# Delta-rule loop of a hybrid decoder trunk: the hand-written order changed around the gated halves, the bonus, the weight rows and the last two tiles

## The chip, the cores and the metric

The kernel runs on one core of a Trainium2 chip. The core has a matrix engine (PE, TensorE), whose weight loads the profile lists apart as PEld, and three engines for elementwise work: DVE (VectorE), ACT (ScalarE) and POOL (GpSimd). SP (SyncE) issues nearly all transfers between the main memory and the on-chip SBUF. PE writes into PSUM banks, which DVE and ACT empty. Each engine works through its own list of instructions in order, and semaphores hold an instruction until what it reads is there. The metric is the device time in microseconds (us) of one execution.

## The reference

Two layers act on x (1024 tokens by 1024 channels, float32). The first is an RWKV-7 time mixer: after projections, a state of 64 by 64 for each of 16 heads is carried over all tokens by a delta rule, its outputs are normalised by head, a bonus is added, and the sum is gated and projected. The second layer is a differential attention; each layer ends with a gated per-layer input. The part that the change touches:

```python
def step(state, inp):
    r_t, w_t, k_t, v_t, kk_t, b_t = inp
    sa = jnp.einsum('bhij,bhj->bhi', state, kk_t)
    state = (state * w_t[:, :, None, :] - sa[..., None] * b_t[:, :, None, :]
             + v_t[..., None] * k_t[:, :, None, :])
    y_t = jnp.einsum('bhij,bhj->bhi', state, r_t)
    return state, y_t
...
y = (y - mean) * lax.rsqrt(var + GN_EPS) * ln_w + ln_b
y = (y + bonus).reshape(B, S, RW_WIDTH)
return (y * jax.nn.silu(gate)) @ w_out
```

## The kernel before, in words

Every matrix product keeps float32 accuracy by splitting both operands into a rounded half ("h") and a rest ("l") and running three matmuls (`mm3`: h by h, h by the weight's l, l by the weight's h). `split` makes the halves: ACT writes the rounded one, then DVE or POOL subtracts it from the source.

The delta rule is run in 16 chunks of 64 tokens, by a loop over c near the end of the function `trunk`. In a chunk PE multiplies the state (tiles `xy`), ACT copies the result to `x`, PE makes `u`, DVE makes `vu` from it, PE makes `s`, DVE adds it to the decayed state (`state`), and PE finishes `xy`, from which ACT copies the outputs `y`. The next chunk's operands are prepared beside it by two units (st 0 and 1): transfers `kkr` and `kb` bring them in, POOL multiplies (`kbp`, `pr`, and a mask on half of `m`), PE transposes (`kbt`) and multiplies (`pm`, `prt`), ACT and DVE empty PSUM (`kbn`, `m`, `bon`). A unit's `kb` buffer is loaded again once POOL's `pr` has read it.

What fills PE between these small products are dense pieces: in chunks 0 to 3 a projection of the per-layer input (`pps`), later the output projection of a finished tile of 128 tokens (`op`), in eight pieces of six matmuls, four pieces a chunk. They are handed out by `more()`. A tile is two chunks. Its steps are spread over the chunks that follow: in an even chunk load, mean (`norm`), square, `bonus_v` (POOL, tile `vn`); in the odd chunk sums, roots, `scaled` (DVE, then POOL's `y<-y,lnw`), `added` (DVE's `y<-y,vn`, the bonus), and `turn(0)` (PE transposes half the tile into `ytr`, DVE gates it into `sg`); in the next even chunk `turned` (ACT rounds `gh<-sg`, DVE makes `gl`), `turn(1)` and `turned` again, and then the first `op` pieces, which read `gh` and `gl`. The eight rows of the output weight are split inside the loop too (`wo_row`: a transfer `rwoNr`, ACT's `rwoNh`, DVE's `rwoNl`).

While the loop is written, `pin` is set: PE, DVE, ACT and POOL keep the order of the code. SP, and everything after the loop, is placed by a scheduler, which may also put later, unpinned instructions between pinned ones. After the loop come the steps of the last two tiles (6 and 7), the gate weights' rows (`pwg`), and the first normalised tile of the next stage (`n`, transposed into `ptr`), whose products are `pg`. All operations are recorded through a wrapper at line 50, so tiles and not lines tell them apart.

Of the kernel before, what the change touches and what calls it, by code (L numbers as in the profile page):

```python
# [37 lines left out]
def trunk(ctx: ExitStack, tc: tile.TileContext, A, out):  # L38
# [814 lines left out]
    def big(kt, x, nm, dt=F32R):  # L853
        return dw.tile([P, D], dt, tag=f"b{kt}{x}", name=nm, bufs=1)

    with NB("d") as d, NP("psco") as pp:
# [55 lines left out]
        def chain_u(c):  # L912
            vu2, px, spl, x = ctx_c[0]
            ti = tis[c // 4]
            pu = [pp.tile([P, 4, 2, L], F32, tag="us", name=f"u{st}_{c}", bufs=2) for st in range(2)]
            ms = []
            if True:
                for p_ in range(4):
                    for h in range(2):
                        for st in (1, 0):  # L920
                            xs_ = half_(st)
                            ms.append(T.matmul(pu[st][xs_, p_, h], lhsT=ti[xs_, (c % 4) * 8 + h * 4 + p_],
                                               rhs=x[xs_, h, p_], start=True, stop=True))
            turns(ms)
            for st in range(2):
                xs_ = half_(st)
                V.tensor_tensor(out=vu2[xs_, st], in0=pu[st][xs_],
                                in1=rn[xs_, c].rearrange("p h j -> p j h").unsqueeze(3).to_broadcast([64, 4, 2, L]),
                                op=ALU.mult)
# [23 lines left out]

        D1, wo = {}, {}

        def wo_row(kt):
            tags = ("sq", "xr", (6, 0), (6, 1), "sq", "xr", (7, 0), "sq")
            tg, nm = tags[kt], f"rwo{kt}r"
            r = dt_(tg, nm) if isinstance(tg, str) else big(*tg, nm, F32)
            nc.sync.dma_start(out=r, in_=A["rwo"][:, kt])  # L960
            h, lo = big(kt, 0, f"rwo{kt}h"), big(kt, 1, f"rwo{kt}l")
            split(h, lo, r, V)
            wo[kt] = (h, lo)
# [123 lines left out]
        for c in range(NCH):  # L1087
# [23 lines left out]
            unit("load", 0, 1)  # L1111
            if odd and w:
                w["sums"]()
            chain_x(c)
            unit("decayed", 0)
            if pj and not odd:
                pj["turned"]()
                pj["turn"](1)
            if w and odd:
                w["roots"]()  # L1120
# [7 lines left out]
                wo_row(0)  # L1128
            if c == 2:
                wo_row(5)  # L1130
            chain_u(c)
            if w:
                w["scaled" if odd else "load"]()
# [6 lines left out]
            unit("pr", 0, 1)  # L1140
            if c == 1:
                wo_row(1)
            chain_s(c)
            if c == 1:
                wo_row(4)
            if c == 3:
                more(9)
                for kt in (2, 3, 6, 7):
                    wo_row(kt)
            if w and not odd:  # L1150
                w["squares"]()
                w["bonus_v"]()
            more(2)
            unit("turn", 1)
            if w and odd:
                w["added"]()
                w["turn"](0)
            more(9)
            unit("bonus", 1)
            if c == 12:  # L1160
                early_raw()
            if c == 13:
                early_row(0)
                early_row(1)
        for e in engines:
            e.pin = False
        co_cm.__exit__(None, None, None)
# [70 lines left out]
            for f in pieces:  # L1238
                f()

        t6, t7 = tile_(NT - 2), tile_(NT - 1)
        tile_(NT - 3)["squares1"]()
        t6["turned"]()
        t6["turn"](1)
        t6["turned"]()
        run(t6["m0"])
        run([t7[nm] for nm in ("load", "norm", "squares", "bonus_v", "sums", "roots", "scaled", "added")])
        while len(wg) < 6:
            gate_w()
        run(t6["m1"])  # L1250
        t6["squares1"]()
        pre2(0)
        gate_w()
# [463 lines left out]
```

## Time and profile before

| what | value |
|---|---|
| median of three runs | 1818.96 us (1814.44 to 1821.0) |
| the profiled execution's own time | 1819.65 us |
| its span, first to last instruction | 1817.8 us |
| mean granted PE clock over the span | 0.959 |
| PE busy in the span | 1683.5 us (93%) |
| the loop over chunks in the profile | from 575 to 882 us |

The span and the time lie 1.85 us apart. A stretch in which PE has nothing in flight is idle time, listed in brackets behind the instruction that ended it with the name of what it waited for. The granted clock is 1.00 at 2.4 GHz and 0.50 at 1.2 GHz; a mean between them over a stretch says how much of it ran at either. A window's row gives its bounds, its length, the busy time of PE, PEld, DVE, ACT and POOL (with the number of instructions), the mean granted clock, and the DMA engines' share and rate.

### The profile page before, as it was taken

To read this page: it belongs to the slowest core of one execution; us is meant where nothing else is said; L and a number is where in the kernel's file an instruction comes from. 1 tells how busy PE (TensorE), PEld (TensorE's weight loads), DVE (VectorE), ACT (ScalarE), POOL (GpSimd) and SP (SyncE) were. 2 spreads that over 40 slices of the span, in tenths; PEclk is the share of its full clock that TensorE was granted. 3 is DMA by queue.
4 is the path that set the end of the run, shared out by engine and by line. 5 is a ranking of instruction groups with operands and counts; after the bars stand their busy time and mean duration, and the time that the engine had idled before them with its cause. 6 is when DMAs were issued, how large, how long until landed. Compare 5 with 4: busy or idle time off the path is not lost.

```text
span 1817.8 us, 31112 instructions
## 1 busy us (share of the span) xinstructions
PE 1683.5 (93%) x11768; PEld 1393.4 (77%) x11768; DVE 1268.2 (70%) x2910; ACT 799.4 (44%) x1690; POOL 608.4 (33%) x647
## 2 busy tenths in 40 slices
PE   6899999898999979898799899899999999999998
PEld 5677778887677867777678678788888888777786
DVE  7865846697993556555856737787877878856765
ACT  6567733246254433334424334444444444544332
POOL 4433635123324444546400332333323323321200
PEclk9999999998898979999899999999999999999999
DMA  7115544534226643353533310101101101431122
GB/s 260 50 54 163 149 116 99 139 100 113 64 74 191 184 137 117 122 164 95 196 116 116 126 35 30 53 24 38 56 7 56 53 10 56 155 99 34 59 93 70
DMA packets 164403, 176.02 MB, mean 97 GB/s; under 512 B 74845, under 2 KB 127837, under 8 KB 164254
## 3 DMA queue, kind: packets, MB, share of 16 engines
q1 hardware_dynamic: 161950, 169.84, 30.2%
q10 hardware_dynamic: 2304, 4.20, 0.6%
q8 instruction: 93, 1.52, 0.3%
q14 instruction: 56, 0.46, 0.1%
HBM read 124.19 MB, written 49.81 MB: 96 GB/s over the span
## 4 chain that ended last, share of the span: by engine, by line
PE 53%; DVE 7%; ACT 1%; DMA 1%; issue 1%; POOL 0%; SPq 0%; DVEq 0%; ACTq 0%; POOLq 0%
PE qkv L50 18%; PE fg L50 5%; PE do L50 4%; PE pg L50 4%; PE op L50 4%; PE sc L50 4%; PE av L50 3%; PE xy L50 2%; PE pm L50 2%; PE at L50 1%; DVE ost L50 1%; PE qkt L50 1%; DVE aT L50 1%; PE u L50 1%; PE s L50 1%
## 5 line engine op out<-in xcount | busy, mean ns | idle before, releaser
L50 ACT ACTIVATE e<-sc,mx 128x256 f32<-128x256 f32 (+7 forms) x128 | 94.1, 739 | 110.7 <-DVE mx L50 59.6
L50 POOL TENSOR_TENSOR rp<-rp,rq 128x128 f32<-128x128 f32 x128 | 61.8, 504 | 230.4 <-DVE rq L50 187.0
L50 PE MATMUL sc<-k,q 128*128 128x512 f32 (+2 forms) x384 | 88.7, 363 | 3.8 <-ACT e L50 2.2
L50 PE MATMUL av<-vh,aT 128*128 128x128 f32 x576 | 82.0, 283 | 6.3 <-DVE aT L50 6.3
L50 PEld LDWEIGHTS av<-vh,aT 128*128 128x128 f32 x576 | 76.3, 197 | 12.8 <-DVE aT L50 8.9
L50 POOL TENSOR_TENSOR m<-m,mmask 128x512 f32<-128x512 f32 x32 | 41.9, 1311 | 112.3 <-ACT m L50 112.3
L50 DVE TENSOR_REDUCE mxs<-sc 128x1 f32<-128x128 f32 (+6 forms) x112 | 73.9, 680 | 0.5
L50 PEld LDWEIGHTS sc<-k,q 128*128 128x128 f32 x384 | 63.2, 190 | 12.9 <-ACT e L50 3.0
L50 PE MATMUL pg<-pwg,ph 128*128 128x512 f32 x224 | 72.3, 401 | 0.2 <-ACT ph L50 0.2
L50 PE MATMUL do<-dwo,oh 128*128 128x512 f32 x224 | 71.7, 401 | 0.8 <-DVE h L50 0.5
L50 DVE SCALAR_TENSOR_TENSOR xmt<-hT,cB,xmt 128x512 f32<-128x512 f32 x64 | 63.6, 1010 | 6.1 <-ACT xmt L50 5.8
L50 ACT ACTIVATE o<-av,r 128x128 f32<-128x128 f32 x64 | 23.5, 368 | 91.0 <-PE av L50 91.0
L50 DVE TENSOR_TENSOR tm<-tb,nb 128x31 f32<-128x31 f32 (+15 forms) x124 | 56.0, 452 | 3.6
L50 DVE SCALAR_TENSOR_TENSOR e<-e,r,e 128x128 f32<-128x128 f32 (+3 forms) x64 | 56.7, 886 | 1.2
L50 POOL CAST q<-q 64x128 fp32r<-64x128 f32 x128 | 38.8, 304 | 52.2 <-PE sc L50 48.1
L50 DVE TENSOR_TENSOR tb<-tb,tm 128x31 f32<-128x31 f32 (+15 forms) x124 | 53.0, 428 | 3.6
L50 POOL CAST k<-k 64x256 fp32r<-64x256 f32 x64 | 25.7, 401 | 86.5 <-ACT k L50 83.5
L50 DVE TENSOR_TENSOR rp<-qkv,rc 128x256 f32<-128x256 f32 x64 | 27.0, 421 | 38.2 <-PE qkv L50 35.5
L50 DVE COPY aT<-at 128x512 f32<-128x512 f32 (+2 forms) x96 | 51.8, 549 | 1.1 <-PE at L50 0.4
L50 PE MATMUL at<-ident,e 128*128 128x128 f32 x288 | 47.4, 277 | 3.1 <-DVE e L50 2.6
L50 DVE SCALAR_TENSOR_TENSOR ost<-ost 128x2 f32<-128x2 f32 x192 | 47.4, 247 | 3.8
L50 DVE TENSOR_TENSOR m<-pm,mmask 128x512 f32<-128x512 f32 x32 | 22.1, 691 | 39.8 <-PE pm L50 37.5
(1136 smaller groups left out, 5610.3 us busy)
## 6 DMA issues: line engine op xcount, KB each, us to landing
pp_d<-ppo SPq DMA_DIRECT2D x32, 256.0 KB, 2.7
kb_d<-kb SPq DMA_DIRECT2D x16, 512.0 KB, 3.3
kkr<-kkr_d SPq DMA_DIRECT2D x32, 256.0 KB, 3.4
kb<-kb_d SPq DMA_DIRECT2D x32, 256.0 KB, 3.1
x<-in_x SPq DMA_DIRECT2D x8, 512.0 KB, 5.6
kkr_d<-ep SPq DMA_DIRECT2D x16, 256.0 KB, 2.6
kkr_d<-rt SPq DMA_DIRECT2D x16, 256.0 KB, 2.6
bb<-kb_d SPq DMA_DIRECT2D x32, 128.0 KB, 2.9
```

The source lines that it names most:

```text
L50: r = f(*a, **k)
```

## The change

In the loop five things move. In even chunks the first `turned` goes ahead of `chain_x`, so ACT has `gh` before the `x` copies. In odd chunks `added` goes from behind the dense pieces to right behind `chain_s`, so DVE has it behind `state`. The rows of the output weight are loaded by a function of their own (`wo_load`) and split at other places: rows 2 and 3 at the end of chunk 3, rows 6 and 7 inside chunk 4, where all four stood at the end of chunk 3. In chunk 15 both halves of tile 6 are turned with one dense piece ahead of each. And the steps of tile 7 and the first half of tile 6's projection are written out, with the pin still set, instead of left to the scheduler.

```diff
+        wo_raw = {}
+
+        def wo_load(*kts):
+            tags = ("sq", "xr", (6, 0), (6, 1), "sq", "xr", (7, 0), "sq")
+            for kt in kts:
+                tg, nm = tags[kt], f"rwo{kt}r"
+                wo_raw[kt] = dt_(tg, nm) if isinstance(tg, str) else big(*tg, nm, F32)
+                nc.sync.dma_start(out=wo_raw[kt], in_=A["rwo"][:, kt])
+
         def wo_row(kt):
-            tags = ("sq", "xr", (6, 0), (6, 1), "sq", "xr", (7, 0), "sq")
-            tg, nm = tags[kt], f"rwo{kt}r"
-            r = dt_(tg, nm) if isinstance(tg, str) else big(*tg, nm, F32)
-            nc.sync.dma_start(out=r, in_=A["rwo"][:, kt])
+            r = wo_raw.pop(kt)
...
+            if pj and not odd:
+                pj["turned"]()
             chain_x(c)
             unit("decayed", 0)
             if pj and not odd:
-                pj["turned"]()
                 pj["turn"](1)
...
+            if c == 4:
+                wo_row(6)
             chain_u(c)
...
             if c == 1:
                 wo_row(1)
+                wo_load(4, 5)
+            if c == 3:
+                wo_load(2, 3, 6, 7)
+            if c == 4:
+                wo_row(7)
             chain_s(c)
+            if c == 0:
+                wo_load(0, 1)
             if c == 1:
                 wo_row(4)
-            if c == 3:
-                more(9)
-                for kt in (2, 3, 6, 7):
-                    wo_row(kt)
...
+            if w and odd:
+                w["added"]()
+            if c == NCH - 1:
+                more()
+                w["turn"](0)
+                w["turned"]()
+                more()
+                w["turn"](1)
+                w["turned"]()
             more(2)
             unit("turn", 1)
-            if w and odd:
-                w["added"]()
+            if w and odd and c < NCH - 1:
                 w["turn"](0)
             more(9)
             unit("bonus", 1)
+            if c == 3:
+                wo_row(2)
+                wo_row(3)
...
+        t6, t7 = tile_(NT - 2), tile_(NT - 1)
+        m0, m1 = list(t6["m0"]), list(t6["m1"])
+        t7["load"]()
+        t7["norm"]()
+        tile_(NT - 3)["squares1"]()
+        m0.pop(0)()
+        t7["squares"]()
+        t7["bonus_v"]()
+        m0.pop(0)()
+        t7["sums"]()
+        m0.pop(0)()
+        t7["roots"]()
+        t7["scaled"]()
+        for f in m0:
+            f()
+        t7["added"]()
         for e in engines:
             e.pin = False
...
-        t6["turned"]()
-        t6["turn"](1)
-        t6["turned"]()
-        run(t6["m0"])
-        run([t7[nm] for nm in ("load", "norm", "squares", "bonus_v", "sums", "roots", "scaled", "added")])
...
-        run(t6["m1"])
+        run(m1)
```

On DVE, from the end of chunk 3 into chunk 4, the list of before reads as follows (`state` closes chunk 3's chain, `y<-y,vn` is `added`, `sg<-ytr` gates a transposed half):

```order
L50 TENSOR_TENSOR state<-s_6296,spl_6198 128x512
L50 TENSOR_TENSOR rwo2l<-rwo2r,rwo2h 128x1024
L50 TENSOR_TENSOR rwo3l<-rwo3r,rwo3h 128x1024
L50 TENSOR_TENSOR rwo6l<-rwo6r,rwo6h 128x1024
L50 TENSOR_TENSOR rwo7l<-rwo7r,rwo7h 128x1024
L50 TENSOR_TENSOR y_5475<-y_5475,vn_6029 128x1024
L50 SCALAR_TENSOR_TENSOR sg_6031<-ytr_6365,vecs,sg_6031 128x128 x4
```

The list of the change at the same place:

```order
L50 TENSOR_TENSOR state<-s_6304,spl_6198 128x512
L50 TENSOR_TENSOR y_5475<-y_5475,vn_6029 128x1024
L50 SCALAR_TENSOR_TENSOR sg_6031<-ytr_6349,vecs,sg_6031 128x128 x4
L50 TENSOR_TENSOR rwo2l<-rwo2r,rwo2h 128x1024
L50 TENSOR_TENSOR rwo3l<-rwo3r,rwo3h 128x1024
L50 TENSOR_TENSOR gl_6342<-sg_6031,gh_6341 128x512
L50 SCALAR_TENSOR_TENSOR sg_6031<-ytr_6435,vecs,sg_6031 128x128 x4
L50 TENSOR_TENSOR m_5_6380<-pm_5_6451,mmask 128x512
L50 TENSOR_TENSOR gl_6342<-sg_6031,gh_6341 128x512
L50 TENSOR_TENSOR rwo6l<-rwo6r,rwo6h 128x1024
L50 TENSOR_TENSOR vu_6162<-u_4_6470,rn 64x512
```

The bonus and the first gating stand ahead of rows 2 and 3; row 6 stands ahead of chunk 4's `vu`, and row 7 (below the piece shown) ahead of chunk 4's `state`.

On ACT, at the start of the even chunk 6 (`bon` closes chunk 5's preparation, `x` copies the chunk's first product), the list of before:

```order
L50 COPY bon<-prt_6_6811 64x8 x2
L50 COPY x_6873<-xy_6838 64x512 x2
L50 ACTIVATE gh_6800<-sg_6496 128x512
L50 COPY m_7_6825<-pm_7_6897 128x512
L50 ACTIVATE gh_6800<-sg_6496 128x512
```

And of the change:

```order
L50 COPY bon<-prt_6_6811 64x8 x2
L50 ACTIVATE gh_6780<-sg_6492 128x512
L50 COPY x_6875<-xy_6840 64x512 x2
L50 COPY m_7_6825<-pm_7_6897 128x512
L50 ACTIVATE gh_6780<-sg_6492 128x512
```

The first rounded half has passed the `x` copies. The same holds in chunks 4, 8, 10, 12 and 14; in chunk 14 four gate-weight activations stand ahead of both, before and after. On DVE the end of chunk 5 reads, before:

```order
L50 TENSOR_TENSOR state<-s_6743,spl_6652 128x512
L50 TENSOR_TENSOR xr_6033<-op_6671,xr_6033 128x512
L50 TENSOR_TENSOR y_5924<-y_5924,vn_6494 128x1024
L50 SCALAR_TENSOR_TENSOR sg_6496<-ytr_6802,vecs,sg_6496 128x128 x4
L50 TENSOR_TENSOR gl_6801<-sg_6496,gh_6800 128x512
```

And with the change:

```order
L50 TENSOR_TENSOR state<-s_6743,spl_6652 128x512
L50 TENSOR_TENSOR y_5926<-y_5926,vn_6490 128x1024
L50 TENSOR_TENSOR xr_6033<-op_6671,xr_6033 128x512
L50 SCALAR_TENSOR_TENSOR sg_6492<-ytr_6802,vecs,sg_6492 128x128 x4
L50 TENSOR_TENSOR gl_6781<-sg_6492,gh_6780 128x512
```

The bonus no longer stands behind `xr<-op`, which waits for the chunk's dense pieces. SP's list changes with it: from chunk 7's loads on, the next `vn` transfer (which waits for `added`) stands ahead of the two `kb` transfers, where it stood behind them.

## Rows read from the trace of the kernel before

**Rows 1.** The page: busy time by engine, and the chain that ended last.

```profile
PE 1683.5 (93%) x11768; PEld 1393.4 (77%) x11768; DVE 1268.2 (70%) x2910; ACT 799.4 (44%) x1690; POOL 608.4 (33%) x647
...
PE 53%; DVE 7%; ACT 1%; DMA 1%; issue 1%; POOL 0%; SPq 0%; DVEq 0%; ACTq 0%; POOLq 0%
```

**Rows 2.** Windows by chunk: chunks 3 to 6, 14, 15 with tail.

```profile
631.48:656.75 25.27, 14.54 (x232) 12.33 (x233) 17.73 (x30) 10.94 (x18) 14.22 (x10) 0.84 0.60 189
656.75:679.35 22.60, 21.72 (x247) 18.25 (x245) 10.48 (x18) 7.09 (x13) 7.96 (x6) 0.72 0.27 79
679.35:697.36 18.01, 16.44 (x247) 13.89 (x245) 11.01 (x23) 5.12 (x11) 11.66 (x10) 1.00 0.32 93
697.36:717.03 19.67, 18.27 (x248) 14.90 (x244) 11.46 (x19) 7.89 (x15) 9.03 (x7) 0.91 0.51 162
...
848.31:870.10 21.79, 18.25 (x249) 15.07 (x245) 11.40 (x19) 12.23 (x19) 14.89 (x10) 0.92 0.30 97
870.10:909.10 39.00, 29.34 (x212) 23.01 (x209) 32.91 (x63) 15.87 (x21) 13.63 (x7) 0.78 0.58 203
```

**Rows 3.** PE groups, chunks 5 to 14: busy, mean ns, idle before.

```profile
L50 PE MATMUL ytr<-ident,y 128*128 128x128 f32 x40 | 7.2, 307 | 8.7 <-DVE y L50 8.7
...
L50 PE MATMUL op<-rwo0h,gh 128*128 128x512 f32 x10 | 5.0, 498 | 7.8 <-ACT gh L50 7.8
```

**Rows 4.** Timeline, end of chunk 3: start, duration, idle before in brackets.

```profile
643.45 1.04 POOL L50 TENSOR_TENSOR kbp<-kb,plast 128x512 f32<-128x512 f32 x1
...
645.68 2.39 POOL L50 TENSOR_TENSOR pr<-kkr,kb 128x256 f32<-128x256 f32 x2
...
652.28 1.22 DVE L50 TENSOR_TENSOR rwo7l<-rwo7r,rwo7h 128x1024 fp32r<-128x1024 f32 x1 [1.12 <-ACT rwo7h L50]
...
654.78 1.09 PE L50 MATMUL ytr<-ident,y 128*128 128x128 f32 x4 [9.57 <-DVE y L50]
```

**Rows 5.** Timeline, end of the odd chunk 5.

```profile
688.98 2.37 POOL L50 TENSOR_TENSOR y<-y,lnw 128x1024 f32<-128x1024 f32 x1 [1.84 <-DVE y L50]
...
691.31 1.05 POOL L50 TENSOR_TENSOR kbp<-kb,plast 128x512 f32<-128x512 f32 x1
...
693.57 1.42 POOL L50 TENSOR_TENSOR pr<-kkr,kb 128x256 f32<-128x256 f32 x2
...
694.88 1.21 DVE L50 TENSOR_TENSOR y<-y,vn 128x1024 f32<-128x1024 f32 x1
694.95 2.06 POOL L50 TENSOR_TENSOR spl<-state,plast 128x512 f32<-128x512 f32 x1
...
696.24 0.63 PE L50 MATMUL ytr<-ident,y 128*128 128x128 f32 x4 [1.57 <-DVE y L50]
```

**Rows 6.** Timeline, start of the even chunk 6.

```profile
696.90 1.12 DVE L50 SCALAR_TENSOR_TENSOR sg<-ytr,vecs,sg 128x128 f32<-128x128 f32 x4 [0.81 <-PE ytr L50]
...
700.54 1.17 ACT L50 COPY x<-xy 64x512 f32<-64x512 f32 x2 [2.73 <-PE xy L50]
701.74 0.63 ACT L50 ACTIVATE gh<-sg 128x512 fp32r<-128x512 f32 x1
702.40 0.69 DVE L50 TENSOR_TENSOR gl<-sg,gh 128x512 fp32r<-128x512 f32 x1 [4.37 <-ACT gh L50]
```

**Rows 7.** Timeline, chunk 14: the last gate-weight activation, and PE's first piece.

```profile
851.97 1.06 ACT L50 ACTIVATE pwg<-pwg0raw 128x1024 fp32r<-128x1024 f32 x1
...
854.93 0.50 PE L50 MATMUL op<-rwo0h,gh 128*128 128x512 f32 x1 [2.95 <-ACT gh L50]
```

**Rows 8.** Timeline, chunk 15 and the tail.

```profile
883.00 2.38 POOL L50 TENSOR_TENSOR y<-y,lnw 128x1024 f32<-128x1024 f32 x1 [1.16 <-DVE y L50]
...
888.67 1.94 PE L50 MATMUL ytr<-ident,y 128*128 128x128 f32 x8 [3.35 <-DVE y L50]
...
892.98 0.79 PE L50 MATMUL op<-rwo0h,gh 128*128 128x512 f32 x1 [2.37 <-ACT gh L50]
...
909.10 1.03 PE L50 MATMUL ptr<-ident,n 128*128 128x128 f32 x8
```

More of the change, by code (lines that the diff above doesn't have):

```diff
@@ L1239, in run @@
                 f()
-        t6, t7 = tile_(NT - 2), tile_(NT - 1)
-        tile_(NT - 3)["squares1"]()
-        t6["turned"]()
-        t6["turn"](1)
-        t6["turned"]()
-        run(t6["m0"])
-        run([t7[nm] for nm in ("load", "norm", "squares", "bonus_v", "sums", "roots", "scaled", "added")])
         while len(wg) < 6:
             gate_w()
-        run(t6["m1"])
+        run(m1)
         t6["squares1"]()
```

## The prediction

> **What bounds the kernel now.** I read the page first. PE is busy 93% of the span, and more than half of the chain that ended last is PE's own work [rows 1]: the kernel is a long list of PE work with holes in it, and a change of order is worth the holes that it closes. The windows say where they lie: one window per chunk of the loop, from the first product of a chunk to that of the next [rows 2]. Chunk 5 takes 18.01 us and holds 16.44 us of PE work at full clock. Chunk 6 takes 19.67 us for the same pieces; PE is busy 18.27 us in it, because the granted clock averages 0.91, so 18.27 - 16.44 = 1.83 us goes to a spell at 1.2 GHz and 19.67 - 18.27 = 1.40 us is idle. Chunk 3 has 25.27 us for 14.54 us of work, chunk 4 runs at a mean clock of 0.72. The last window, chunk 15 and the tail up to the next stage's first transposes, has 39.00 us with PE busy for 29.34.
>
> The groups of PE's instructions name the two repeated holes [rows 3]. In chunks 5 to 14 PE stands 8.7 us before `ytr` for DVE's `y` (once in each of five odd chunks: 1.57 us in chunk 5 [rows 5]; if three others are like it, one has 2.4) and 7.8 us before the first `op` matmul for ACT's `gh` (once in each of five even chunks). The timelines show why. In chunk 5 `y<-y,vn` starts on DVE at 694.88, although POOL's `lnw` product, which it needs, ended at 688.98 + 2.37 = 691.35 [rows 5]: it queues behind an instruction that waits for the dense pieces. In chunk 6 `sg` is gated by 696.90 + 1.12 = 698.02, but ACT rounds it at 701.74, behind the `x` copies, which wait for PE [rows 6]. At the end of chunk 3 four weight rows keep DVE until 652.28 + 1.22, and `ytr` comes 9.57 us late [rows 4].
>
> **The change, part by part.** *Weight rows and chunk 3.* PE would be ready for `ytr` at 654.78 - 9.57 = 645.21 [rows 4]. `added` no longer waits for rows 2, 3, 6 and 7, but POOL is then in `kbp` until 643.45 + 1.04 = 644.49. Chunk 5's end shows what happens when DVE's bonus and a POOL product of this size overlap: `spl`, started 0.07 us after the bonus, took 2.06 us, where `kbp` of the same shape took 1.05; the later one stood about 1.01 us [rows 5]. The Trainium skill ("SBUF — State Buffer", section "Who interferes with whom") speaks against this change here: a DVE operation with both inputs in SBUF and a POOL operation that reads SBUF exclude each other, and the one that issues second stands for the whole of the other. By that rule `spl` would have stood the 1.14 us of the overlap (694.88 + 1.21 less 694.95), and each sum below would change by 0.1 us.
>
> So I put `added` from 644.5 to 645.7, and `ytr` at 645.7 to 646.35 (0.63 us at full clock, as in rows 5). Next late is POOL: its mask product stands behind the bonus, and then `pr` takes 1.42 us when undisturbed [rows 5], after a mask product of 1.21 us (the 693.57 - 691.31 from `kbp` to `pr`, less `kbp`'s 1.05). `pr` ends near 648.4, and `prt`, which reads it, ends near 649.0. Chunk 3 then ends at 649.0 and not at 656.75: 7.7 us. Chunk 4 keeps its 16.44 us of PE work and gets new waits, since rows 2 and 3 stand ahead of `gl`, row 6 ahead of `vu`, and row 7 ahead of `state` on DVE. Behind two rows of 1.22 us, `gl` comes about 0.6 us after PE wants it; behind `gl` and row 6, `vu` about 1.0 us after PE has done all that stands ahead of `s`; and the `op` piece that reads row 7 about 1.2 us late, since a mean over a tile and the row lie ahead. That is 19.2 us, and with half of a 1.83 us clock loss about 20.2, against 22.60 [rows 2]: 2.4 us. Together 10.1 us. The bounds: 8 if each of the three waits is doubled (2.8 us more, with 0.7 less of the clock loss), 12 if there are none but half of one.
>
> *The bonus in odd chunks.* `ytr` follows `kbt` without the 1.57 us. But the bonus now starts at about 691.4, in the middle of POOL's `kbp`, mask, `pr` [rows 5]. One of them stands, so `pr`, which ended at 693.57 + 1.42 = 694.99, ends about 1.1 us later, at 696.1. PE finishes `ytr` at 694.67 + 0.63 = 695.30 and stands 0.8 us before `prt`. What was a wait of 1.57 for DVE becomes one of 0.8 to 0.9 for POOL: 0.7 us a chunk is left, four times, and 2.4 - 0.9 = 1.5 in the longer one: 4.3 us. If `pr` isn't held up, it is the full 8.7; if the `vn` transfer, now ahead of `kb` in SP's list, delays the `kb` loads too, I take 2. I cost that transfer at nothing: it waits for a bonus that ends by 693.5, and the `kb` load behind it waits for the first half of `pr` anyway, until 694.3 (half of 1.42 after 693.57) or later.
>
> *The rounded halves in even chunks.* `gh` can run at 698.0 to 698.7, on an ACT that is idle until 700.54; the `x` copies don't move [rows 6]. The `gh` wait goes: 7.8 - 2.95 = 4.85 us in chunks 6, 8, 10 and 12 [rows 3, 7]. In chunk 14 ACT is busy with gate weights until 851.97 + 1.06 = 853.03; `gh` can start there, not at 854.24 behind the copies, so 1.2 of the 2.95 us goes [rows 7]. Sum 6.0 us, bounds 4.5 (half of chunk 14's, and a new wait for `gl` in each) to 6.8.
>
> *The clock.* I take chunk 6's 1.83 us at 1.2 GHz [rows 2] for chunks 8, 10 and 12 too. The rows show that it follows idle time among small products: chunk 5, with one hole, stays at 1.00, chunk 6, with a second one soon after, doesn't. With one smaller hole a pair in place of two I expect half the spells to go: 4 x 1.83 / 2 = 3.7 us; bounds 0 and 7.3.
>
> *The tail.* Chunk 15 keeps its stretch up to POOL's `lnw`, which ends at 883.00 + 2.38 = 885.38, since the gate rows that delay it stay where they are. Then `added` comes at once (no longer behind tile 7's mean): `ytr` near 886.7 and not 888.67 [rows 8]. But a dense piece of six matmuls is now held behind each `ytr`, so PE's hole ahead of it grows from 3.35 to about 4.5 us. After it, ACT still has two gate-weight activations of 1.06 us [rows 7] ahead of `gh`, and `gl` may stand for a gate product on POOL, of the size of `lnw` (2.38 us). I get the last `op` piece at 906 to 908 where `ptr` stands at 909.10: 2 us, bounds 0 and 5. The next stage was dense behind it, so what is gained stays.
>
> **Sum.** 10.1 + 4.3 + 6.0 + 3.7 + 2.0 = 26.1 us. The profiled execution took 1819.65 us (span 1817.8 and 1.85 around it), so 1793.5; its own time lies 0.7 us above the median of 1818.96, and I give 1793. The upper bounds make 12 + 8.7 + 6.8 + 7.3 + 5 = 39.8 us (1780), the lower ones 8 + 2 + 4.5 + 0 + 0 = 14.5 us (1805).
>
> **Rivals.** *All holes close and the clock stays up* (1780 to 1787). For it: PE has work for every hole, POOL is only 33% busy [rows 1]. Against: in odd chunks POOL has no gap between `lnw` and `spl` [rows 5]. Chance 0.19.
>
> *The port takes most of it back* (1800 to 1808, about 1803). The bonus beside POOL turns the `ytr` wait into a `prt` wait of nearly its size, the spells of low clock stay because a hole stays, and the tail's gain goes into the wait for `gl`: 4.3 + 3.7 + 2.0 fewer, 16.1 us gained. For it: `spl`'s 2.06 us. Against: the pair of holes becomes one. Chance 0.13.
>
> *The change doesn't do what it says* (1814 to 1823): the moved instructions were not the ones PE waits for. Against: rows 3 name them; the order shows them moved. Chance 0.05.
>
> *Slower, by the clock* (about 1843). Transposes, `prt` and `xy` now follow each other with little dense work between, and PE may stay at 1.2 GHz for whole chunks. Chunk 4 shows the price: at a clock of 0.72 it is busy 21.72 us, 5.3 more than chunk 5 [rows 2]. If chunks 4 to 14 all ran so, 11 x 5.3 = 58 us, less 5.3 + 5 x 1.83 = 14.5 already paid, less the 20.4 us that the first three parts give: 23 us slower. It decides from seven such chunks (34.9 / 5.3 = 6.6). Against: chunk 5 at 1.00. The Trainium skill ("TensorE: Matmul & The Clock Gate", section "A second HAM failure mode: psum-queue depth-cycling") tells of a kernel whose short PE pauses made the clock go up and down; chunks 6 and 14 agree, with 0.91 and 0.92. Chance 0.03.
>
> **Numbers.** The forecast has 0.60, with a range of its own of 1787 to 1800. 1780 to 1805 takes in most of the first two rivals and leaves out little more than the last two: over 8 in 10. About 0.5% (9 us) is what a measurement of this kernel can tell from no change; forecast and the first two rivals are faster by more (0.92), the third is the same (0.05), the last slower (0.03).
>
> **What the profile would show.** Right: no 9.57 us hole at the end of chunk 3, which is then 17 to 18 us; odd chunks near 17.3 us with PE waiting not for `y` but about 0.8 us for POOL's `pr` before `prt`; `op` waiting for `gh` in chunk 14 alone, even chunks of 16.5 us (clock 1.00) or 18.3 (0.91); `ytr` in the tail near 16.6 us after chunk 15's first product. Wrong: `pr` undisturbed and odd chunks at 16.5 (too little forecast), or chunk 4 above 22 us with `s` waiting for `vu`, or a `kb` load that holds `pm`.

## The result and the profile after

The changed kernel took 1794.34 us (median of four runs, 1792.27 to 1797.27), against 1819.18 us before in the same runs: a ratio of 0.9861, 95% interval [0.9841, 0.9881]. Run again with five rounds, beside other runs of the kernel before, it gave 0.9876 [0.9852, 0.9901]. The forecast was 1793, in a range of 1780 to 1805.

The page of the changed kernel, busy time by engine, answers to [rows 1]:

```profile
span 1790.4 us, 31127 instructions
...
PE 1676.9 (94%) x11768; PEld 1391.3 (78%) x11768; DVE 1272.1 (71%) x2910; ACT 798.9 (45%) x1690; POOL 609.0 (34%) x647
```

The span fell by 27.4 us. PE's busy time fell by 6.6 us for the same 11768 instructions, which goes with the clock (a mean of 0.964 over the span, 0.959 before); the other 20.8 us are holes that closed. This execution is the fastest of its four: by the medians the gain is 24.8 us. The windows by chunk answer to [rows 2]: chunks 3 to 6, then 12 and 14, then chunk 15 with the tail.

```profile
631.04:648.23 17.19, 14.03 (x232) 11.83 (x232) 12.37 (x26) 6.94 (x14) 10.85 (x9) 1.00 0.69 220
648.23:671.00 22.77, 19.91 (x247) 16.78 (x245) 17.56 (x20) 10.67 (x17) 10.15 (x10) 0.85 0.49 138
671.00:688.23 17.23, 16.57 (x248) 14.10 (x245) 11.58 (x25) 5.12 (x11) 9.91 (x9) 1.00 0.26 79
688.23:707.48 19.25, 19.25 (x247) 16.31 (x245) 10.23 (x16) 7.92 (x15) 9.42 (x8) 0.82 0.53 162
794.65:810.86 16.21, 16.21 (x247) 13.88 (x245) 10.23 (x16) 7.92 (x15) 9.43 (x8) 1.00 0.77 232
828.09:849.83 21.74, 19.79 (x246) 16.30 (x245) 12.73 (x16) 11.99 (x19) 15.14 (x10) 0.84 0.42 133
849.83:883.60 33.77, 26.55 (x212) 21.08 (x208) 25.82 (x54) 16.12 (x21) 12.15 (x6) 0.90 0.67 234
```

Chunk 3 is 8.1 us shorter, chunk 4 no shorter. Chunk 6 is full (PE is busy all of its 19.25 us) and still long, because its mean clock is 0.82, lower than before; chunk 12 has the same work at 1.00 in 16.21 us. Chunk 14 is as long as before. PE's groups over chunks 5 to 14 show the two repeated holes of [rows 3] gone and a smaller one in their place:

```profile
L50 PE MATMUL prt<-rk,pr 128*64 128x2 f32 x164 | 7.8, 200 | 3.3 <-POOL pr L50 1.7 <-ACT kbn L50 1.6
L50 PE MATMUL ytr<-ident,y 128*128 128x128 f32 x40 | 7.8, 326 | 0.0
L50 PE MATMUL op<-rwo0h,gh 128*128 128x512 f32 x10 | 5.5, 548 | 0.0
```

The timeline at the end of the odd chunk 5 shows where `prt`'s wait comes from; it answers to [rows 5]:

```profile
682.96 1.06 POOL L50 TENSOR_TENSOR kbp<-kb,plast 128x512 f32<-128x512 f32 x1
...
683.04 2.06 DVE L50 TENSOR_TENSOR y<-y,vn 128x1024 f32<-128x1024 f32 x1 [0.25 <-POOL y L50]
683.97 2.27 POOL L50 TENSOR_TENSOR m<-m,mmask 128x512 f32<-128x512 f32 x1
...
686.20 1.42 POOL L50 TENSOR_TENSOR pr<-kkr,kb 128x256 f32<-128x256 f32 x2
...
687.09 0.25 PE L50 MATMUL prt<-rk,pr 128*64 128x2 f32 x2 [0.33 <-ACT kbn L50]
...
687.67 0.63 PE L50 MATMUL prt<-rk,pr 128*64 128x2 f32 x14 [0.34 <-POOL pr L50]
```

The bonus starts with `lnw` done. It starts 0.08 us behind `kbp`, ends about 1.1 us after it, and takes 2.06 us in place of 1.21; then the mask product waits out the bonus and takes 2.27 in place of the 1.28 that it takes a few microseconds earlier in the same chunk. That puts `pr` 1 us later, and the second part of `prt` waits 0.34 us for it.

Chunk 4's two holes in the timeline:

```profile
660.00 2.07 DVE L50 TENSOR_TENSOR rwo6l<-rwo6r,rwo6h 128x1024 fp32r<-128x1024 f32 x1
...
662.72 1.41 PE L50 MATMUL s<-vu,kbn 128*64 128x64 f32 x32 [1.08 <-DVE vu L50]
...
664.94 1.92 POOL L50 TENSOR_TENSOR vn<-vn,bon 128x1024 f32<-128x1024 f32 x1
...
665.28 1.61 DVE L50 TENSOR_SCALAR gst<-gst 128x16 f32<-128x16 f32 x1
...
668.07 1.22 DVE L50 TENSOR_TENSOR rwo7l<-rwo7r,rwo7h 128x1024 fp32r<-128x1024 f32 x1
...
669.34 0.50 PE L50 MATMUL op<-rwo7l,gh 128*128 128x512 f32 x1 [1.74 <-DVE rwo7l L50]
```

Both holes are in good part POOL's. Row 6 takes 2.07 us, where row 7 takes 1.22: POOL's `kbp` runs beside it (from 659.48, 1.50 us). And a step of tile 1's mean ahead of row 7, on 16 columns, takes 1.61 us beside `vn`, where the same step takes 0.18 at 671.96.

Chunk 14's hole: the first rounded half is early now, but DVE's `gl` runs beside POOL's gate products:

```profile
830.65 4.69 POOL L50 TENSOR_TENSOR pwg<-pwg0raw,pwg 128x1024 fp32r<-128x1024 f32 x2 [3.18 <-ACT pwg L50]
...
833.26 2.63 DVE L50 TENSOR_TENSOR gl<-sg,gh 128x512 fp32r<-128x512 f32 x1 [5.47 <-ACT gh L50]
...
835.95 0.52 PE L50 MATMUL op<-rwo0h,gl 128*128 128x512 f32 x1 [1.93 <-DVE gl L50]
```

And the tail, which answers to [rows 8]:

```profile
866.57 0.67 PE L50 MATMUL ytr<-ident,y 128*128 128x128 f32 x4 [2.85 <-DVE y L50]
...
883.60 1.57 PE L50 MATMUL ptr<-ident,n 128*128 128x128 f32 x8 [2.09 <-DVE n L50]
```

### The profile page after: what moved, and what is told of

Read it like the earlier page. It is cut to its first block, busy times and chain, and to the rows that moved or that the text cites. A ratio compares the mean times of both kernels' runs of the same rounds, so it can differ in the third digit from the quotient of the medians.

```text
span 1790.4 us, 31127 instructions
## 1 busy us (share of the span) xinstructions
PE 1676.9 (94%) x11768; PEld 1391.3 (78%) x11768; DVE 1272.1 (71%) x2910; ACT 798.9 (45%) x1690; POOL 609.0 (34%) x647
## 4 chain that ended last, share of the span: by engine, by line
PE 63%; DVE 25%; issue 4%; ACT 4%; POOL 3%; DMA 1%; SPq 0%; ACTq 0%; DVEq 0%; POOLq 0%
PE qkv L50 18%; PE d L50 7%; PE fg L50 5%; PE pg L50 5%; PE do L50 4%; PE sc L50 3%; DVE xmt L50 3%; PE xy L50 3%; PE av L50 3%; DVE tm L50 3%; PE op L50 3%; DVE tb L50 3%; DVE nb L50 2%; DVE ost L50 2%; PE pm L50 1%
## 5 line engine op out<-in xcount | busy, mean ns | idle before, releaser
L50 POOL TENSOR_TENSOR m<-m,mmask 128x512 f32<-128x512 f32 x32 | 47.9, 1496 | 81.7 <-ACT m L50 81.7
```

The lines of the kernel that those rows point to most:

```text
L50: r = f(*a, **k)
```

## The experiments

My theory was that each part is worth the hole that it closes, and that half of the low-clock spells go with the holes. The rivals: POOL takes the gain back, because its operations and DVE's hold each other up; the parts only work in pairs; and the clock does something else. Ratios below are to the kernel before, run on the same chip. Gaps and chunk lengths are of one profiled execution each.

### The parts alone

**The halves alone** (in even chunks, the first rounded half ahead of the `x` copies):

```diff
+            if pj and not odd:
+                pj["turned"]()
             chain_x(c)
             unit("decayed", 0)
             if pj and not odd:
-                pj["turned"]()
                 pj["turn"](1)
```

> The kernel before with one edit alone: in even chunks the first rounded half stands ahead of the x copies. My theory (each hole is worth its own length, and the clock spell of an even chunk follows its idle hole): the op matmuls no longer wait for gh in chunks 6, 8, 10 and 12 (4.85 us), and since the second hole of each pair is gone, half or more of the four spells go too (3.7 to 7): 8 to 12 us faster, even chunks at 16.5 to 18.3 us, odd ones unchanged at 18.0. Rival (the clock falls for the pair, hole of the odd chunk and stretch of small products, so it recovers only if the bonus moves too): even chunks stay at a clock of 0.91 and near 18.3 us, 4 to 6 us faster.

Measured: 1816.29 us, ratio 0.9974 [0.9963, 0.9985]. The windows of chunks 6, 8, 10 and 12:

```profile
695.83:713.57 17.74, 17.74 (x249) 15.28 (x245) 11.57 (x19) 7.90 (x15) 9.02 (x7) 0.90 0.54 172
731.58:750.90 19.32, 19.32 (x249) 16.83 (x245) 11.56 (x19) 7.90 (x15) 8.92 (x7) 0.82 0.48 155
770.50:790.74 20.24, 20.24 (x247) 17.39 (x245) 10.51 (x18) 7.92 (x15) 7.96 (x6) 0.78 0.38 122
808.76:828.03 19.27, 19.27 (x248) 16.30 (x244) 11.57 (x19) 7.89 (x15) 9.02 (x7) 0.82 0.56 172
```

PE has no hole left in them, and they are 76.6 us together, against 77.9 before (19.67, 19.71, 19.34, 19.18): 1.3 us from 4.85 us of holes. The clock took the rest, with means of 0.78 to 0.90 where chunk 6 had 0.91 [rows 2]. My theory was too high. The ratio is worth 4.7 us (2.7 to 6.7), which lies in the rival's range, but not where the rival has it: the even chunks come to 19.1 us on average, not 18.3, and chunk 4, which the windows don't show, is 2.1 us shorter. The spells did not follow the idle time of the even chunk itself; the wait of 1.57 us at the end of the odd chunk ahead was still there.

**The bonus alone** (`added` right behind `chain_s` in odd chunks):

```diff
+            if w and odd:
+                w["added"]()
             more(2)
             unit("turn", 1)
             if w and odd:
-                w["added"]()
                 w["turn"](0)
```

> The kernel before with one edit alone: in odd chunks the bonus stands right behind the state on DVE. My theory: odd chunks go from 18.0 to 17.2 us and chunk 9 from 19.0 to 17.2, five chunks 4.9 us, with PE waiting 0.3 to 0.8 us for POOL's pr ahead of prt in place of 1.57 for y; even chunks keep their gh hole of 1.2 to 1.4 us. The chunk 3 weight rows still stand ahead of the bonus there or take its place behind it: with the bonus ahead of them, part of chunk 3's 9.57 us goes into later waits, 0 to 6 us more. In all 5 to 11 us faster. Rival (the port takes it back): POOL's slower products hold prt for as long as y did, under 2 us faster outside chunks 3 and 4.

Measured: 1809.06 us, ratio 0.9937 [0.9924, 0.9949], about 11 us. The odd chunks are 17.21 to 17.23 us, 5.0 us less in all, as my theory had it; chunk 3 is unchanged. The windows of chunks 5, 6 and 8:

```profile
681.17:698.38 17.21, 16.56 (x248) 14.10 (x244) 12.61 (x25) 5.12 (x11) 11.20 (x10) 1.00 0.34 98
698.38:716.50 18.12, 16.73 (x247) 13.82 (x245) 10.13 (x16) 8.02 (x15) 9.41 (x8) 1.00 0.54 166
733.72:753.73 20.01, 19.08 (x247) 15.74 (x245) 10.14 (x16) 8.01 (x15) 9.44 (x8) 0.83 0.51 155
```

Chunk 6 still has its hole of 1.39 us, at full clock. With the halves alone the hole went and the low clock stayed; here, in chunks 6 and 12, it is the other way round. In this profile 2 us of gain are the clock's in chunks 6 to 12 (75.95 against 77.90 with the holes still there), and 3.2 lie in chunk 15 and the tail (35.75 us against 39.00), where the edit also brings forward chunk 15's bonus.

**The weight rows alone** (`wo_load` and the new places of `wo_row`, as in the change's diff):

> The kernel before with one edit alone: the weight rows are loaded apart and split at other places, rows 2 and 3 at the end of chunk 3, row 6 and row 7 inside chunk 4. The bonus of chunk 3 stays behind the dense pieces. My theory (the stretch is worth what the whole change showed there): chunk 3 falls from 25.3 to about 18 us, chunk 4 stays near 22.7, in all 7 to 8 us faster and nothing elsewhere. Rival (the bonus's place was needed as well, so that the hole ahead of ytr stays over 3 us, or the clock spell only moves on): 3 to 5 us.

Measured: 1812.55 us, ratio 0.995 [0.9934, 0.9966]. Chunks 3 and 4:

```profile
631.73:648.91 17.18, 14.03 (x232) 11.82 (x232) 12.37 (x26) 6.93 (x14) 10.82 (x9) 1.00 0.69 219
648.91:673.92 25.01, 21.18 (x247) 17.27 (x245) 17.55 (x20) 10.78 (x17) 10.14 (x10) 0.80 0.44 126
```

Chunk 3 gains all of its 8.1 us, chunk 4 loses 2.4: the holes for `vu` (1.07 us) and row 7 (1.78 us) are there as in the full change, with 0.94 us for `gh` on top. Net 5.7 us in the two. The rest lies in the tail, 35.8 us in place of 39.0, where the scheduler came to another order: tile 7's `lnw` product stands ahead of a gate product on POOL.

**The tail alone** (chunk 15's pieces and the last two tiles written out, as in the change's diff):

> The kernel before with one edit alone: chunk 15's dense pieces and the steps of the last two tiles written out. My theory (the tail's gain is its own): the loop up to chunk 14 is unchanged, chunk 15 and the tail fall from 39.0 to about 33.8 us, and 1 to 2 us more come behind it, since the next stage's first rows are issued earlier: 5 to 7 us faster. Rival (the tail gained because the chunks ahead of it ran earlier against a fixed time of transfers and gate rows): under 3 us, with the gates' weight rows ending the waits.

Measured: 1813.69 us, ratio 0.996 [0.9944, 0.9975]. Chunk 15 and the tail:

```profile
870.09:902.59 32.50, 26.36 (x213) 20.87 (x209) 24.46 (x53) 16.11 (x21) 9.46 (x6) 0.89 0.67 243
```

6.5 us shorter than the 39.00 before [rows 2]. Of these 3.5 are idle time (9.66 to 6.14) and 3.0 PE's busy time, that is clock. Nothing ahead of it had moved, so the gain is the edit's own. But the tail of before, in the same order, took 41.4 us in the profile of the halves alone, with 3.43 us of wait for `gh` and 2.59 for `gl` in place of 2.37 and 1.75: one profile says the tail's length to some 2 us only.

The four ratios make 0.26 + 0.63 + 0.50 + 0.40 = 1.79% (by their intervals, added in squares, give or take 0.28), the whole change 1.39% [1.19, 1.59] and 1.24% [0.99, 1.48]. All four ratios share the runs of before, so 0.28 is a little too small. On the whole the parts don't need each other, but the sum hides two differences that the profiles show, one profile of each kernel. In chunk 15 and the tail the bonus, the rows and the tail edit each take time off alone (3.3, 3.2 and 6.5 us), and the whole change takes off only 5.2: these gains overlap, and chunk 15's bonus is moved by two of the edits. In chunks 6 to 12 it is the reverse: the halves take off 1.3 us and the bonus 1.9, the change 7.0 and, in a second profile below, 10.1. There the two do work as a pair; the pair without the rows and the tail was not run.

### The clock

**The changed kernel once more**, unaltered:

> The changed kernel, unaltered, profiled and timed a second time. My theory on the clock (where a spell of 1.2 GHz falls is decided by how the run happens to lie in time, not by the holes): the same chunks keep the same lengths of work and the same holes to within 0.1 us, but other even chunks run at 1.00 and others at 0.82 or 0.91 than in the first profile, and the span differs by 1 to 5 us through that alone. Rival (the order of instructions decides the spell): chunk 6 at 0.82, chunks 8 and 10 at 0.90 and chunk 12 at 1.00 once more.

Measured: 1795.17 us. Chunks 6, 8, 10 and 12 of its profile:

```profile
688.70:704.92 16.22, 16.22 (x246) 13.87 (x245) 10.22 (x16) 7.92 (x15) 9.43 (x8) 1.00 0.61 189
722.15:739.86 17.71, 17.71 (x247) 15.28 (x246) 10.23 (x16) 7.93 (x15) 9.42 (x8) 0.90 0.56 173
757.09:773.29 16.20, 16.20 (x248) 13.87 (x246) 10.90 (x16) 7.76 (x15) 9.40 (x8) 1.00 0.58 180
790.50:808.21 17.71, 17.71 (x246) 15.28 (x244) 10.21 (x16) 7.92 (x15) 9.42 (x8) 0.90 0.69 209
```

The same instructions in the same order ran chunk 6 at 1.00 and chunk 12 at 0.90, where the first profile had 0.82 and 1.00; the holes of chunks 3 to 5 agreed within 0.03 us, and only chunk 14 waited 1.5 us more, for `gh`. So the order of the instructions doesn't fix the place of a spell, and below I call it chance. These four chunks took 70.9 us in one profile and 67.8 in the other, while the spans came to 1790.4 and 1790.6, since 2.6 us went the other way behind the tail.

**A dense piece between `ytr` and `prt`** in odd chunks:

```diff
-            more(2)
+            more(1 if w and odd else 2)
             unit("turn", 1)
```

> The changed kernel with one edit: in odd chunks one dense piece of six matmuls stands between ytr and prt. Hole by hole: prt no longer waits (0.67 us), ytr comes 1.4 us earlier and waits 0.3 to 0.5 us for the bonus: odd chunks 16.9 us, 1.5 us in all. Theory A on the clock (a spell of 1.2 GHz follows a long run of small products, idle or not): the run from kbt to chunk 6's first op piece is cut in two, so the spells in chunks 6, 8, 10 and 12 go: 4 to 5 us more. Theory B (spells fall by chance of position wherever PE does small products): spells stay, in other places, and 1 to 2 us is all.

Measured: 1794.26 us, 0.9866 [0.9845, 0.9888]: no change. The odd chunks stayed at 17.2 us: `prt` waited 0.2 us and not 0.66, but `ytr`, now earlier by the length of the piece, waited 0.3 us for the bonus, and PE's busy time was 0.2 us longer. The four even chunks had one spell in the profile, and the mean clock over the timed runs was 0.963 against the change's 0.961.

**A piece held back into the even chunk.** Joined with the edits below, and there compared with that kernel:

```diff
+                if odd and c < NCH - 1:
+                    held.append(dense.pop())
...
             unit("decayed", 0)
+            if held and not odd:
+                held.pop()()
```

> The first kernel of this list with one more edit: the last dense piece of each odd chunk is held back and stands between xy and ytr at the start of the next even chunk, so that the run of small products there is cut in front of ytr. Hole by hole this costs about 1 us in each odd chunk, where ytr and prt come 1.4 us earlier and wait for the bonus and pr. Theory A on the clock (spells follow long runs of small products): no spell begins in chunks 6, 8, 10 and 12, and the mean clock over the timed runs is higher by 0.002 or more (2 us and above). Theory B (spells come wherever small products fall, by chance of position): the mean clock is the same within 0.001 and the kernel 3 to 5 us slower.

Measured: 1805.64 us, 0.9919 [0.9886, 0.9951], against 0.9804 [0.9784, 0.9823] without the edit, and a mean clock over the timed runs of 0.958 against 0.969. One of its six executions took 1788.62 us, at a clock of 0.970. Chunks 6 and 7:

```profile
686.74:707.46 20.72, 20.72 (x253) 17.61 (x251) 10.97 (x18) 7.92 (x15) 9.42 (x8) 0.84 0.54 172
707.46:724.00 16.54, 15.34 (x242) 12.96 (x238) 12.41 (x24) 5.12 (x11) 11.22 (x10) 1.00 0.27 75
```

All of chunks 6, 8, 10, 12 and 14 have a spell here, none of them without the edit, and no PE instruction was added. Neither theory said that. What the edit did to PE: without it a dense piece stands between `kbt` and `ytr`; with it `kbt`, a hole of 0.86 us, `ytr`, a hole of 0.34, `prt` and both `xy` follow one another before the next dense piece. The table sets this stretch, from the last dense matmul (128x512) of one chunk to the first of the next, at full clock, beside the spells at the start of chunks 6, 8, 10 and 12:

| kernel | gap, us | of it idle, us | chunks with a spell |
|---|---|---|---|
| all, ahead of odd chunks 7 to 13 | 3.94 | 0 | none |
| the three joined kernels below, where no wait is left | 4.6 to 4.8 | 0 to 0.2 | 0 of 11 |
| a dense piece between `ytr` and `prt` | 4.4 | 0.2 | 1 of 4 |
| `kbp` first (below) | 5.2 | 0.33 | 1 of 4 |
| the change, twice, and with rows behind (below) | 5.75 | 0.66 | 8 of 12 |
| a piece held back | about 5.8 | 1.2 to 1.4 | 4 of 4 |
| the last kernel below, chunk 6 | 6.0 | 1.2 | 0 of 1 |
| the bonus alone | 7.4 | 1.6 to 2.1 | 2 of 4 |
| the halves alone | 6.8 and more | 1.6 and more | 4 of 4 |
| before, and with the tail alone | 8.2 and more | 2.5 and more | 8 of 8 |
| the rows alone | 8.2 and more | 2.5 and more | 3 of 4 |

(The 5.8 is the 4.64 of the joined kernel with `kbt` in place of the `ytr` behind `xy`, and 1.2 us of holes; the 6.8 is the 8.2 of before less 1.4.) On the whole the spells get more frequent with the gap, small products and idle time together, and where in a run they fall is chance. That is a relation over thirteen kernels that differ in other things too, with exceptions (the bonus alone, the last kernel's chunk 6), and not a cause that was shown: length and idle time grow together here. The pair with and without the held piece is the cleanest of it. The Trainium skill ("TensorE: Matmul & The Clock Gate", section "A second HAM failure mode: psum-queue depth-cycling") puts such up and down to short pauses of PE. The halves alone disagree in so far as their even chunks, with no pause in them, ran at 0.78 to 0.90; the pause of 1.57 us lay in the gap ahead.

### What the new waits cost, and a faster kernel

**The second unit's `kbp` ahead of `lnw`** on POOL in odd chunks, into the gap of 1.84 us:

```diff
             chain_u(c)
-            if w:
-                w["scaled" if odd else "load"]()
+            if w and not odd:
+                w["load"]()
             unit("turn", 0)
             unit("decayed", 1)
+            if w and odd:
+                w["scaled"]()
```

> The changed kernel with one edit: in odd chunks POOL gets the second unit's kbp ahead of the lnw product, where it stands idle for 1.84 us. My theory (prt waits for pr because POOL has no gap from lnw to spl): pr ends about 1 us earlier, the 0.34 us that prt waits for pr go in chunks 5, 7, 9, 11 and 13 and the 0.33 for kbn stay: odd chunks 16.9 us, 1.7 us in all, more in chunk 3 is not to be had since it has no lnw work beside it. Rival (bonus and mask product then start together and one waits out the other): the bonus ends up to 1.1 us later, ytr waits instead and odd chunks stay at 17.2 or get longer.

Measured: 1785.56 us, 0.9818 [0.9794, 0.9841], some 10 us less than the change run beside it. The end of chunk 5:

```profile
678.74 1.05 POOL L50 TENSOR_TENSOR kbp<-kb,plast 128x512 f32<-128x512 f32 x1
680.95 2.38 POOL L50 TENSOR_TENSOR y<-y,lnw 128x1024 f32<-128x1024 f32 x1 [1.16 <-DVE y L50]
683.28 1.30 POOL L50 TENSOR_TENSOR m<-m,mmask 128x512 f32<-128x512 f32 x1
683.36 2.30 DVE L50 TENSOR_TENSOR y<-y,vn 128x1024 f32<-128x1024 f32 x1 [0.57 <-POOL y L50]
...
687.09 0.63 PE L50 MATMUL prt<-rk,pr 128*64 128x2 f32 x16 [0.33 <-ACT kbn L50]
```

The wait for `pr` is gone. The bonus still waits, now for the mask product, but ends early enough. Odd chunks are 16.66 us (5 x 0.57 = 2.9 us less) and chunk 3 loses 0.7, since it has the same POOL work after all. That is 3.6 us by chunk lengths at full clock; the rest goes with the clock, whose mean over the timed runs is 0.967 against 0.961. By my expectation 1.7 us were to be had: the chunks gave twice that, and the clock I had not counted.

**Row 6 behind `vu`, row 7 and the mean behind the state** in chunk 4:

```diff
-            if c == 4:
-                wo_row(6)
             chain_u(c)
+            if c == 4:
+                wo_row(6)
...
-            if w and not odd:
+            if w and not odd and c != 4:
                 w["norm"]()
...
-            if c == 4:
-                wo_row(7)
             chain_s(c)
+            if c == 4:
+                wo_row(7)
+                w["norm"]()
```

> The changed kernel with one edit in chunk 4: weight row 6 goes behind vu on DVE, row 7 and the mean of tile 1 behind state. My theory (chunk 4's two holes are these rows): s no longer waits 1.08 us for vu; the op matmuls that read row 7's rest still wait up to 1.7 us for it, since it stays the last thing DVE makes there: chunk 4 at 21 to 22 us in place of 22.8, 1 to 2 us faster. Rival (a hole moved is a hole kept): the op matmuls wait 2.8 us for row 7, no gain.

Measured: 1796.6 us, 0.9883 [0.9863, 0.9903], no difference from the change's 0.9876. The hole for `vu` went, that for row 7 stayed at 1.78 us, and a spell began behind it: chunk 5 came to 20.60 us at a clock of 0.82.

**Joined.** `kbp` first; in odd chunks a dense piece between `kbt` and `ytr`; row 6 behind `vu` and row 7 ahead of the mean; and the early gate rows by ACT's scaled rounding and one DVE operation, not on POOL:

```diff
-            more(2)
+            more(1 if w and odd else 2)
             unit("turn", 1)
+            more(1 if w and odd else 0)
...
-        EG = (G, G)
+        EG = (None, None)
```

> The changed kernel with the second unit's kbp ahead of lnw in odd chunks, and three more edits, each in other chunks: in odd chunks a dense piece between kbt and ytr, in chunk 4 row 6 behind vu and row 7 ahead of the mean, and the two early gate rows scaled straight into their rounded halves with the rest on DVE instead of POOL. Mine: odd chunks 16.3 to 16.4 us (prt no longer waits for kbn), chunk 4 without its holes of 1.08 and 1.75 us (about 20 us at its clock of 0.85), chunk 14 without the waits for gh and gl (18 to 19 us): against the kernel with the kbp edit alone 1.6 + 2.8 + 3.5, about 7 us faster, a ratio of 0.977 to 0.979 to the kernel before. Rival (the clock takes it): with fewer holes the granted clock falls in more chunks, as it did when the halves were moved alone, and less than 3 us is left.

Measured: 1780.13 us, 0.9804 [0.9784, 0.9823], 5.4 us less than with `kbp` first by the medians of two sessions, but 2.5 by the two ratios, whose intervals overlap; 7 were expected. Chunks 4 to 7 and 14:

```profile
646.98:668.82 21.84, 19.40 (x247) 16.87 (x245) 16.48 (x20) 9.91 (x16) 10.05 (x9) 0.84 0.50 144
668.82:686.90 18.08, 18.07 (x244) 15.37 (x244) 12.38 (x25) 5.86 (x12) 10.88 (x9) 0.91 0.17 47
686.90:703.11 16.21, 16.21 (x247) 13.88 (x245) 10.77 (x19) 8.02 (x15) 9.47 (x8) 1.00 0.72 220
703.11:719.66 16.55, 16.54 (x249) 14.06 (x245) 12.53 (x24) 5.11 (x11) 11.23 (x10) 1.00 0.20 58
818.19:835.93 17.74, 16.50 (x247) 13.80 (x245) 14.53 (x21) 9.87 (x17) 9.84 (x8) 1.00 0.52 163
```

Chunks 6 to 13 have almost no idle time (0.2 us, in chunk 9) and no spell. Chunk 14 is 4 us shorter with POOL out of DVE's way. In chunk 4 the two holes became one of 2.44 us: the state, now behind row 7 and the mean.

**A third projection piece in chunk 3** (`n = (4, 5, 4, 3)`), on top:

> The kernel before this one in the list with one more edit: one projection piece of the per-layer input (six matmuls, about 1.4 us at full clock) is moved from chunk 0, which has no hole, to the end of chunk 3. Mine: chunk 3 keeps its length and the 1.4 us lie in its hole of 2.3 to 2.6 us ahead of ytr, chunk 0 gets 1.4 us or more shorter: 1.5 us faster. Rival: chunk 0 is not bound by PE and chunk 3's copies out of PSUM delay the bonus: no change or 1 us slower.

Measured: 1786.43 us, 0.9823 [0.9809, 0.9836], 6 us slower by the medians; the intervals just overlap, but the profile has chunk 4 longer by 4.8 us. The piece closed 1.4 us of chunk 3's holes, as expected, and chunk 3 kept its length. But the rows 2 and 3 are loaded over buffers that the projection's operands hold, so their transfers now stand behind the third piece, and in SP's list behind a `kb` load as well. They were issued at 645.89, where the joined kernel has 638.39, and chunk 4's `op` waited:

```profile
655.29 0.79 PE L50 MATMUL op<-rwo0h,gh 128*128 128x512 f32 x1 [5.49 <-ACT gh L50]
```

ACT's `gh` stands behind `rwo3h`, which waits for its row. A cost in neither expectation.

**The mean behind the state, and the second gate row later**, on top of the joined kernel:

```diff
+            if c == 14:
+                early_row(1)
...
-            if w and not odd:
+            if w and not odd and c != 4:
                 w["norm"]()
...
             chain_s(c)
+            if c == 4:
+                w["norm"]()
...
                 early_row(0)
-                early_row(1)
```

> The joined kernel with two more edits: in chunk 4 the mean of tile 1 stands behind the state on DVE, and the second early gate row is made in chunk 14 behind the gating instead of ahead of it. Mine: the 2.44 us in which chunk 5's first product waits for the state go, and the spell of 1.2 GHz behind them in chunk 5 (1.5 us) with them; the 1.24 us in which chunk 14's pieces wait for gl go: 4 to 5 us faster than the joined kernel, a ratio of 0.977 to 0.979 to the kernel before. Rival (the mean is the late thing): squares and sums of tile 1 come later and chunk 5's bonus with them, so the hole moves to chunk 5's ytr and 1 us or less is left.

Measured: 1777.31 us, 0.979 [0.9765, 0.9816]: the fastest by 2.8 us of the medians, though its interval overlaps that of the joined kernel. Chunk 14 is 16.6 us. Chunks 4 and 5:

```profile
644.35:663.70 19.35, 19.35 (x247) 16.84 (x245) 14.02 (x18) 9.25 (x15) 10.13 (x8) 0.82 0.51 143
663.70:682.79 19.09, 16.88 (x248) 13.97 (x244) 16.58 (x28) 6.51 (x12) 12.33 (x10) 1.00 0.22 65
```

Chunk 4 has no hole left; 2.17 us are back in chunk 5, 0.85 of them ahead of `ytr`, because tile 1's mean, square and sums come later. The rival was half right.

## Why the prediction came out right, step by step

- **Weight rows, 10.1 us predicted, 7.9 measured** (8.1 in chunk 3, a loss of 0.2 in chunk 4). Chunk 3 went as worked out from [rows 4], where 7.7 were put. The step that failed is "with half of a 1.83 us clock loss about 20.2" for chunk 4. The three waits were to be 2.8 us and are 2.82, which is luck: the one for `gl` didn't come, and the other two (1.08 and 1.74) hold 0.85 and 1.4 us of waiting for POOL that the prediction doesn't have in chunk 4. The clock was 0.85, that is 19.91 - 16.44 = 3.5 us lost where I had put 0.9. One of the prediction's own signs of being wrong, chunk 4 above 22 us with `s` waiting for `vu`, came up.
- **The bonus, 4.3 predicted, 4.9 measured** in the five odd chunks, and 5.0 alone. The turn from a wait for `y` into one for `pr` is what happened; its size is 0.66 us a chunk, half of it for `kbn`, where I had 0.8. That POOL's order is the cause of the half for `pr` was shown by putting `kbp` first; the 0.33 us for `kbn` stayed there.
- **The halves and the clock, 4.85 + 3.7 = 8.55 predicted in chunks 6 to 12; 7.0 in the first profile and 10.1 in the second.** The 4.85 us of holes closed. The reason given for the clock, that a spell "follows idle time among small products", was half of it: the halves alone, which took the idle time out of the even chunks, lost the gain to the clock. A spell cost 1.5 us, not 1.83 (chunks 8 and 12 of the second profile against 6 and 10). Alone, the halves gave 1.3 us here and the bonus 1.9, as "one smaller hole a pair in place of two" would have it; the table speaks for the shorter gap ahead of the even chunk, which is argued and not shown. The size is in part luck: two profiles of the same kernel lie 3.1 us apart.
- **Chunk 14, 1.2 predicted, 0.05 measured.** I moved the wait for `gh` and left out what is late next: `gl`, at POOL's gate products, took 2.63 us against 0.69 in [rows 6]. The prediction had that wait in the tail only.
- **The tail, 2.0 predicted, 5.2 measured.** `ytr` came 16.74 us after chunk 15's first product; 16.6 was written. PE's idle time fell from 9.66 to 7.22, 2.4 us; the other 2.8 us are clock, which I had not put there. The hole ahead of `ytr`, which was to grow from 3.35 to about 4.5 us, shrank to 2.85, and the waits for `gh` and `gl` went; 2.09 us ahead of `ptr` came up. Behind the tail another 1.9 us went, which can't be told from chance (from `ptr` to the end the fourteen profiles took 904.9 to 912.8 us).
- **The sum.** 26.1 predicted; 27.4 in the profiles. Too much in chunk 4 and 14 (3.7 us), too little in the tail and behind it (5.1). The mechanisms of the holes were right; that the forecast of 1793 lies 1.3 us from the median is luck, since these errors cancel.
- **The rivals.** "The port takes most of it back" was right in mechanism and wrong in price: the bonus and the mask product each took about 1 us more, and PE felt 0.34 of it a chunk. "All holes close" is what the joined kernels came near to, at 1777 to 1780, once POOL's order was changed too. "Slower, by the clock" showed itself in the held piece, 25 us slower than its partner by the medians.

## What to carry to other kernels

A hole on the matrix engine among small products can have a second price, the clock behind it, and closing one of two holes need not win it back, as the halves alone show. In this kernel it went best with the whole stretch between two dense pieces shortened. Judge by several executions, since where a spell falls is chance. When an operation moves earlier on DVE, look at what POOL does at that moment, and whether POOL has a gap earlier that could take its work. An operation taken off a queue makes the next one late: in chunk 4 row 6, row 7, the mean and the state took turns as the last to come, and the chunk lost its last hole only when all four were ordered by when they are wanted (22.77, 21.84, then 19.35 us), with 2.17 us of waits back in the next one.

## What the runs showed of the hardware

Not expected: how small an operation can be and still wait for POOL. In the changed kernel's tail a product in the working out of a norm's scale, on 6 columns, took 2.34 us beside POOL's `wg7l`, and held up `n` and with it the next stage's first transposes (the 2.09 us ahead of `ptr` above):

```profile
879.97 2.37 POOL L50 TENSOR_TENSOR wg7l<-pwg07r,wg7h 128x1024 fp32r<-128x1024 f32 x1 [4.73 <-ACT wg7h L50]
880.02 2.34 DVE L50 TENSOR_TENSOR rn<-rn 128x6 f32<-128x6 f32 x1
```

The same product beside no POOL work takes 0.16 to 0.17 us. It started 0.05 us behind POOL's and waited for all of it, as the Trainium skill says ("SBUF — State Buffer", section "Who interferes with whom"): the one that issues second waits for the whole of the other. The step on 16 columns in chunk 4 (1.61 against 0.18 us, ending 0.03 us after POOL's `vn`) and the bonus behind `kbp` (2.06 against 1.21 us) agree as well.
